# A Delta-rule layer whose TensorE order is written as chains woven with projections

## The chip, the cores and the metric

The kernel runs on one NeuronCore of a Trainium2 chip. The metric is the device time of one execution in microseconds, the median of several runs. All arithmetic is float32; large products are taken as three products of split operands.

## What is computed

A stack of blocks over x of 512 positions x 1024. The third mixer, a gated Delta-rule layer with 8 heads of 128, is the one that matters:

```python
proj = h @ w_in                            # q, k, v, z: 1024 each; beta, a: 8 each
q, k, v = silu(causal_conv(qkv, w_conv))   # 4 taps
q = q * rsqrt(sum(q * q) + EPS) / sqrt(d); k = k * rsqrt(sum(k * k) + EPS)
beta = sigmoid(beta_logit)
g = -exp(a_log) * softplus(a_logit + dt_bias)
# per head and chunk:
decay = where(causal, exp(g_cum_i - g_cum_j), 0)
L = where(strict, (k_beta @ k.T) * decay, 0); T = inverse(eye + L)
u, w = T @ v_beta, T @ (k_beta * exp(g_cum))
# scan over chunks with a state:
v_new = u - w @ state
o = q_dec @ state + qk @ v_new
state = state * exp(g_last) + k_dec.T @ v_new
# behind the scan: o * rsqrt(mean(o * o) + EPS) * w_onorm, times silu(z), then @ w_out
```

The reference's chunks are 64 long; the kernel works on four of 128 to a head.

## The kernel before

`build` runs the layers one after the other; the order of instructions on each engine comes from a scheduler that works with its own estimates, the code setting the data flow. Tiles are 128 partitions x 512.

**Projections.** `fm` (L346) takes one unit of weights: `mm3` (L328 to L330) issues three matmuls `pj` for each of 8 slices of the contraction, 24 to a unit. The three of one slice are called a k-step here. The layer has one unit of 40 columns (the rates beta and a), then for each of heads 0 to 5 the units k, v, q, z, for heads 6 and 7 k, v, q, and the two z units at the end. Each unit's weights are split on the way: ACT writes `whi` (L222), DVE `wlo` (L223). `pj` has three PSUM banks. All else shares four pools: `pa` (two banks), `pb`, `pc` and `po` (one each).

**One head** in `gdn_layer` (L663 on) goes so:
- A broadcast DMA brings the head's gate row `Gb`; POOL forms `dc`, `dT` (L743, L744), ACT exponentiates them (L749, L750) and `Gb` (L751).
- `conv_silu` for k: DVE multiplies the unit's result by the norm (`u`, L717), four taps (L630, L634), ACT takes silu (L719). TensorE turns it (`kt`, L642), ACT squares (L760), DVE sums (`ssk`), POOL takes the root (`rk`, L659), ACT scales (L765); TensorE turns it back (`knt`), ACT copies `knT` (L768), and TensorE forms `kk` (L771).
- `block_inverses` (L856) inverts the diagonal 16 x 16 blocks: ACT copies four pieces `d`, DVE cuts them down (L868, L870), SP writes them to DRAM (`dd`, L872) and reads them back spread out (`lb`, L875), and DVE sweeps 15 steps of four operations on `tmp` (L882) and `X` (L884).
- v: `conv_silu`, `vt`, scaled by ACT. q: `conv_silu`, the sum of squares `ss` in `sumsq_fm`, and `kq`, which DVE multiplies into `dT` (L791).
- `unit_inverse_T` (L887) joins blocks to 32, 64 and 128: `full` on DVE (L902), `Dt`, `z`, `e`, `dz`, `e`, `dz`, `e` on TensorE, with copies `Dm`, `zt` on ACT between them. It was issued behind the last projection by `tc.issue_after(self.last.ins)`.
- The scan, four chunks: `ks` with the state (L810), `r` on DVE (L812), `vn` (L814), its copy on ACT (L816), `ds` (L819), the new state `S` (L822, L824), the outputs `o` (L826, L827). Then `on` on ACT, and, one head later, `ot` and the gate (`finish`).

Behind the last head come the two z units and `out_proj`, whose own weights follow.

Of the kernel before, what the change touches and what calls it, by code (L numbers as in the profile page):

```python
# [18 lines left out]
P = 128  # L19
S = 512  # L20
# [180 lines left out]
class Stream:  # L201
# [32 lines left out]
    def next(self):  # L234
        while self.done < min(self.pos + 1 + self.look, len(self.plan)):
            self.fetch()
        r = self.ready[self.pos]
        self.ready[self.pos] = None
        self.pos += 1
        return r  # L240


class KB:
# [419 lines left out]
    def gdn_layer(self):  # L663
        nc = self.nc
        self.stage = ("pa", 2)
        self.norm_end()
        h, rb, rc = self.h, self.rb, self.rc
        H = 8
        self.stage = ("pa", 2)
        bps = self.small_fm(40, h)  # L670
        rows = self.big("E", shape=[40, S])
        xb = self.big("E")
        nc.vector.tensor_mul(xb[:40], bps[:40], rb[:40])
        nc.gpsimd.memset(rows, 0.0)
        nc.scalar.activation(rows[:8], xb[:8], AF.Tanh, scale=0.5)
        nc.vector.tensor_scalar(rows[:8], rows[:8], 0.5, 0.5, ALU.mult, ALU.add)
        A = slice(32, 40)
        nc.vector.tensor_scalar_add(xb[A], xb[A], self.col("gdt")[A])
        la, lb = self.big("Gb"), xb
        nc.scalar.activation(la[A], xb[A], AF.Abs)  # L680
        nc.scalar.preload_act_table_set("natural_log_exp_and_others")
        nc.scalar.activation(la[A], la[A], AF.Exp, scale=-1.0)
        nc.scalar.activation(la[A], la[A], AF.Ln, bias=1.0)
        ea = self.small([P, 1], "ea")
        nc.scalar.activation(ea[A], self.col("gal")[A], AF.Exp)
        nc.vector.tensor_scalar_max(lb[A], xb[A], 0.0)
        nc.vector.tensor_add(lb[A], lb[A], la[A])
        nc.vector.tensor_scalar(lb[A], lb[A], ea[A], -1.0, ALU.mult, ALU.mult)
        for t in range(NT):
            c = slice(t * P, (t + 1) * P)  # L690
            nc.vector.tensor_tensor_scan(rows[A, c], self.ones[A], lb[A, c], 0.0, ALU.mult, ALU.add)
        Gb = self.bcast_rows(rows[A], H, "Gb")
        gps = self.att("gc")
        for t in range(NT):
            nc.tensor.transpose(gps[:, t * 40:(t + 1) * 40], rows[:, t * P:(t + 1) * P], self.ident[:40, :40])
        gc = self.small([P, NT, 40], "cols", 1)
        nc.vector.tensor_copy(gc, gps[:, :NT * 40].rearrange("p (t c) -> p t c", t=NT))
        ng = self.small([P, NT, H], "ng", 1)
        nc.vector.tensor_scalar_mul(ng, gc[:, :, 32:40], -1.0)
        nb = self.small([P, NT, H], "nb", 1)  # L700
        nc.vector.tensor_scalar_mul(nb, gc[:, :, 0:8], -1.0)
        nbe = self.small([P, NT, H], "nbe", 1)
        nc.scalar.activation(nbe, gc[:, :, 32:40], AF.Exp)
        nc.vector.tensor_mul(nbe, nbe, nb)
        strict = self.con("strict").unsqueeze(1).to_broadcast([P, NT, P])
        causT = self.con("causT").unsqueeze(1).to_broadcast([P, NT, P])
        v4 = lambda a: a.rearrange("p (t d) -> p t d", t=NT)
# [3 lines left out]
        blk = [slice(t * P, (t + 1) * P) for t in range(NT)]  # L711
        os_, g, NZ = [], [], 2

        def conv_silu(i, hd):
            ps = self.fm(h)
            u = us[(3 * hd + i) % 2]
            nc.vector.tensor_mul(u[:, 3:], ps, rb)  # L717
            y = self.conv_taps(u, "gw", i * 8 + hd, 4, f"y{i}", bufs=3)
            nc.scalar.activation(y, y, AF.Silu)  # L719
            return y, u[:, 3:]  # L720

        late = []

        def finish():

            on, z = late.pop()
            old, self.stage = self.stage, ("pc", 1)
            with self.tc.issue_after(self.last.ins):
                ot = self.t4(on, "ot")
            if z is not None:  # L730
                g.append(self.gate(ot, z, self.col("gon")))
            else:
                o = self.big("o", bufs=NZ)
                nc.scalar.activation(o, ot, AF.Copy, scale=self.col("gon"))
                os_.append(o)
            self.stage = old

        for hd in range(H):
            self.stage = ("pa", 2)

            G = Gb(hd, 2)
# [11 lines left out]
            nc.gpsimd.tensor_copy(eg, v4(G)[:, :, P - 1])  # L753

            kT, sq = conv_silu(1, hd)
            if late:
                finish()
            kps = self.t4(kT, "kt")
# [7 lines left out]
            kps = self.t4(kn, "knt")  # L766
            knT = self.big("knT", bufs=3)
            nc.scalar.copy(knT, kps)  # L768
            kk = self.att("kk")
            for t in range(NT):  # L770
                nc.tensor.matmul(kk[:, blk[t]], knT[:, blk[t]], knT[:, blk[t]], start=True, stop=True)  # L771
            for t in range(NT):
                c = blk[t]
                nc.vector.scalar_tensor_tensor(dc[:, c], kk[:, c], nb[:, t, hd:hd + 1], dc[:, c], ALU.mult, ALU.mult)
            X = self.block_inverses(dc)
            nc.gpsimd.tensor_mul(v4(kn)[:, :NT - 1], v4(kn)[:, :NT - 1], kd[:, :NT - 1].unsqueeze(2).to_broadcast([P, NT - 1, P]))

            vT, _ = conv_silu(2, hd)
            vps = self.t4(vT, "vt")
            bv = vT  # L780
            for t in range(NT):
                nc.scalar.activation(bv[:, blk[t]], vps[:, blk[t]], AF.Copy, scale=gc[:, t, hd:hd + 1])

            qT, sq = conv_silu(0, hd)
            e2 = self.small([P, NT], "e2")
            nc.vector.tensor_scalar(e2, self.sumsq_fm(qT, sq), P * EPS, P * EPS * EPS, ALU.mult, ALU.add)
            kq = self.att("kq")
            for t in range(NT):
                nc.tensor.matmul(kq[:, blk[t]], knT[:, blk[t]], qT[:, blk[t]], start=True, stop=True)
            At = dT  # L790
            nc.vector.tensor_mul(At, kq, dT)  # L791
            qd = qT
            nc.gpsimd.tensor_mul(qd, qT, G)
            z = self.silu_z(2) if hd < H - NZ else None
            self.stage = ("pb", 1)
            with self.tc.issue_after(self.last.ins):
                E = self.unit_inverse_T(dc, X)

            self.stage = ("po", 1)
            ops = self.att("o")  # L800
            self.stage = ("pc", 1)
            so = self.small([P, NT], "sso", 2)
            Sx = None
            for t in range(NT):
                c = blk[t]
                if t == 0:
                    rr = bv[:, c]
                else:
                    ks = self.att("ks")
                    nc.tensor.matmul(ks[:, :P], knT[:, c], Sx, start=True, stop=True)  # L810
                    rr = self.small([P, P], "r", 2)
                    nc.vector.scalar_tensor_tensor(rr, ks[:, :P], nbe[:, t, hd:hd + 1], bv[:, c], ALU.mult, ALU.add)  # L812
                vn_ps = self.att("vn")
                nc.tensor.matmul(vn_ps[:, :P], E[:, c], rr, start=True, stop=True)  # L814
                vn = self.small([P, P], "vn", 2)
                nc.scalar.copy(vn, vn_ps[:, :P])  # L816
                if t < NT - 1:
                    ds_ps = self.att("ds")
                    nc.tensor.matmul(ds_ps[:, :P], kn[:, c], vn, start=True, stop=True)  # L819
                    Sn = self.small([P, P], "S", 2)  # L820
                    if t == 0:
                        nc.scalar.copy(Sn, ds_ps[:, :P])  # L822
                    else:
                        nc.vector.scalar_tensor_tensor(Sn, Sx, eg[:, t:t + 1], ds_ps[:, :P], ALU.mult, ALU.add)  # L824
                if t > 0:
                    nc.tensor.matmul(ops[:, c], qd[:, c], Sx, start=True, stop=False)  # L826
# [3 lines left out]
                if t < NT - 1:  # L830
                    Sx = Sn
# [8 lines left out]
            late.append((on, z))  # L840
        finish()
        self.stage = ("pa", 2)
        for o in os_:
            g.append(self.gate(o, self.silu_z(2)))
        self.out_proj(g, "nw3")

    def sumsq_fm(self, src, s):

        nc = self.nc
        nc.scalar.activation(s, src, AF.Square)  # L850
        ps = self.att("ss")
        for t in range(NT):
            nc.tensor.matmul(ps[:, t:t + 1], s[:, t * P:(t + 1) * P], self.ones[:, 0:1], start=True, stop=True)
        return ps[:, :NT]
# [32 lines left out]
    def unit_inverse_T(self, N, X):  # L887
# [3 lines left out]
        nc = self.nc  # L891
        v4 = lambda a: a.rearrange("p (t d) -> p t d", t=NT)
        off = self.small([P, S], "off", 1)
        nc.gpsimd.tensor_mul(v4(off), v4(N), self.con("off16").unsqueeze(1).to_broadcast([P, NT, P]))
        for s in (16, 32, 64):
            X2 = self.big("E", shape=[P, NT, P]) if s == 64 else self.small([P, NT, 2 * s], f"X{2 * s}", 1)
            nc.gpsimd.tensor_scalar_mul(X2[:, :, :s], X, self.con(f"even{s}"))
            if s == 16:
# [4 lines left out]
                                     self.con(f"bd{s}").rearrange("p (b i) -> p b i", i=s).unsqueeze(1).to_broadcast([P, NT, nb, s]))  # L903
                ps = self.t4(full, "Dt")
                Dm = self.small([P, S], "Dm", 1)
                nc.scalar.copy(Dm, ps)
                zp = self.att("z")
# [4 lines left out]
                ep = self.att("e")  # L912
# [3 lines left out]
                nc.vector.scalar_tensor_tensor(X2[:, :, s:], X, self.con(f"odd{s}"), ev, ALU.mult, ALU.add)  # L916
            else:
                nc.scalar.activation(X2[:, :, s:], X, AF.Copy, scale=self.con(f"odd{s}"))
                dz = self.att("dz")
# [10 lines left out]
                ep = self.att("e")  # L930
                for lo, pair in rows:
# [3 lines left out]
                    nc.scalar.copy(X2[lo, :, s:], ep[lo, :w].rearrange("p (t c) -> p t c", t=NT))  # L935
            X = X2
# [597 lines left out]
```

## Time and profile before

| | |
|---|---|
| runs before | 2082.03, 2085.77, 2086.82 us; median 2085.77 |
| profiled execution | 2088.03 us |
| its span | 2086.3 us, mean granted clock 0.989 |
| busy in the span | PE 2026.5, DVE 1213.0, ACT 886.7, POOL 164.3 us |
| the layer on TensorE | 505.7 to 928.0 us, the next layer's norm at its end |

The profile is one execution; the 1.7 us between its time and its span lie around the span. In the trace L12 is line 12 of the kernel; PE is TensorE's matmuls, PEld its weight loads. A view of windows gives the busy time of each engine in a stretch, with the number of instructions, the mean granted clock of TensorE (PEclk, 1.00 is full), and the share of DMA. A releaser behind `<-` is what the waiting instruction waited for last.

The columns of a window are:

```
core 0: us, PE busy (x) PEld busy (x) DVE busy (x) ACT busy (x) POOL busy (x), PEclk, DMA share, GB/s
```

### The profile page before, as it was taken

To read this page: it belongs to the slowest core of one execution; us is meant where nothing else is said; L and a number is where in the kernel's file an instruction comes from. 1 tells how busy PE (TensorE), PEld (TensorE's weight loads), DVE (VectorE), ACT (ScalarE), POOL (GpSimd) and SP (SyncE) were. 2 spreads that over 40 slices of the span, in tenths; PEclk is the share of its full clock that TensorE was granted. 3 is DMA by queue.
4 is the path that set the end of the run, shared out by engine and by line. 5 is a ranking of instruction groups with operands and counts; after the bars stand their busy time and mean duration, and the time that the engine had idled before them with its cause. 6 is when DMAs were issued, how large, how long until landed. Compare 5 with 4: busy or idle time off the path is not lost.

```text
span 2086.3 us, 25930 instructions
## 1 busy us (share of the span) xinstructions
PE 2026.5 (97%) x9810; PEld 1592.0 (76%) x9810; DVE 1213.0 (58%) x2420; ACT 886.7 (43%) x1640; POOL 164.3 (8%) x178
## 2 busy tenths in 40 slices
PE   8999999999899988999999999999999999999999
PEld 6888787777777766778667767776788878888887
DVE  5545445555876765465765546644544467878621
ACT  4222343344776553453565454356622243322211
POOL 0000000000333221100001101000011100000000
PEclk9999999999999997999999999999999999999999
DMA  5233432225322221153114412120232342332331
GB/s 183 92 101 117 137 110 78 85 72 175 87 78 65 65 75 31 52 179 98 50 41 157 123 59 93 61 81 31 71 101 92 99 165 93 99 101 92 111 121 66
DMA packets 64508, 197.69 MB, mean 95 GB/s; under 512 B 8412, under 2 KB 8796, under 8 KB 64384
## 3 DMA queue, kind: packets, MB, share of 16 engines
q1 hardware_dynamic: 63440, 193.57, 28.9%
q0 software_dynamic: 800, 2.25, 0.4%
q8 instruction: 77, 1.26, 0.3%
q14 instruction: 47, 0.39, 0.1%
q10 hardware_dynamic: 144, 0.22, 0.0%
HBM read 183.13 MB, written 12.89 MB: 94 GB/s over the span
## 4 chain that ended last, share of the span: by engine, by line
PE 61%; DVE 5%; ACT 4%; DMA 2%; POOL 2%; issue 1%; POOLq 0%; SPq 0%; ACTq 0%; DVEq 0%
PE pj L330 16%; PE pj L328 16%; PE pj L329 16%; DMA lb<-dd 2%; PE s L1042 1%; PE z L1404 1%; DVE tmp L882 1%; PE o L1095 1%; PE pt L1086 1%; DVE X L884 1%; DVE wlo L223 1%; POOL rk L659 1%; PE dz L926 1%; PE tm L328 0%; PE dz L928 0%
## 5 line engine op out<-in xcount | busy, mean ns | idle before, releaser
L328 PE MATMUL pj<-hh,whi 128*128 128x512 f32 (+2 forms) x1528 | 609.1, 399 | 7.6 <-ACT hh L342 7.6
L329 PE MATMUL pj<-hl,whi 128*128 128x512 f32 (+2 forms) x1528 | 611.2, 400 | 1.2 <-DVE hl L343 1.2
L330 PE MATMUL pj<-hh,wlo 128*128 128x512 f32 (+2 forms) x1528 | 609.3, 399 | 2.0 <-DVE wlo L223 2.0
L222 ACT CAST whi<-raw 128x1024 fp32r<-128x1024 f32 x301 | 313.7, 1043 | 663.9 <-PE pj L329 417.3
L223 DVE TENSOR_TENSOR wlo<-raw,whi 128x1024 fp32r<-128x1024 f32 x301 | 375.5, 1248 | 203.5 <-ACT whi L222 197.2
L328 PEld LDWEIGHTS pj<-hh,whi 128*128 128x128 f32 (+2 forms) x1528 | 288.1, 189 | 68.3 <-ACT hh L342 8.0
L330 PEld LDWEIGHTS pj<-hh,wlo 128*128 128x128 f32 (+2 forms) x1528 | 288.3, 189 | 64.8 <-issue 4.3
L329 PEld LDWEIGHTS pj<-hl,whi 128*128 128x128 f32 (+2 forms) x1528 | 288.4, 189 | 62.7 <-issue 3.6
L328 PE MATMUL pj<-gh,whi 128*128 128x512 f32 x432 | 170.7, 396 | 0.5 <-ACT gh L339 0.3
L329 PE MATMUL pj<-gl,whi 128*128 128x512 f32 x432 | 170.7, 396 | 0.0
L330 PE MATMUL pj<-gh,wlo 128*128 128x512 f32 x432 | 170.6, 396 | 0.0
L634 DVE SCALAR_TENSOR_TENSOR y<-u,cols,y 128x512 f32<-128x512 f32 x160 | 123.0, 769 | 2.4
L328 PEld LDWEIGHTS pj<-gh,whi 128*128 128x128 f32 x432 | 81.0, 188 | 20.4 <-ACT whi L222 1.1
L329 PEld LDWEIGHTS pj<-gl,whi 128*128 128x128 f32 x432 | 81.0, 188 | 18.7 <-DVE gl L340 0.4
L330 PEld LDWEIGHTS pj<-gh,wlo 128*128 128x128 f32 x432 | 81.1, 188 | 18.4 <-DVE wlo L223 0.4
L473 DVE TENSOR_TENSOR x<-pj,x 128x512 f32<-128x512 f32 x48 | 33.1, 691 | 93.9 <-PE pj L330 93.9
L328 PE MATMUL pj<-whi,hh 128*128 128x512 f32 x168 | 66.4, 398 | 0.0
L329 PE MATMUL pj<-wlo,hh 128*128 128x512 f32 x168 | 66.1, 394 | 0.0
L330 PE MATMUL pj<-whi,hl 128*128 128x512 f32 x168 | 65.7, 392 | 0.0
L1435 DVE TENSOR_TENSOR gt<-pj,rb 128x512 f32<-128x512 f32 x24 | 16.5, 690 | 64.1 <-PE pj L330 64.1
L882 DVE TENSOR_TENSOR tmp<-lb,X 128x30 f32<-128x30 f32 (+14 forms) x240 | 43.7, 214 | 11.8 <-DMA lb<-dd 11.8
L1466 DVE TENSOR_TENSOR u<-pj,rb 128x512 f32<-128x512 f32 x44 | 30.5, 693 | 30.5 <-PE pj L330 28.7
(480 smaller groups left out, 2845.1 us busy)
## 6 DMA issues: line engine op xcount, KB each, us to landing
raw<-in_w_dram SPq DMA_DIRECT2D x290, 512.0 KB, 3.5
xd<-x SPq DMA_DIRECT2D x40, 256.0 KB, 2.0
x<-xd SPq DMA_DIRECT2D x40, 256.0 KB, 3.4
x<-in_xT_dram SPq DMA_DIRECT2D x16, 256.0 KB, 3.2
lb<-dd SPq DMA_DIRECT2D x8, 512.0 KB
raw<-in_w4m_dram SPq DMA_DIRECT2D x8, 512.0 KB, 4.0
ncb<-ncb SPq DMA_DIRECT2D x8, 256.0 KB
Gb<-Gb SPq DMA_DIRECT2D x8, 256.0 KB, 3.2
```

The costliest lines, as they stand in the source:

```text
L222: nc.scalar.copy(hi, raw)
L223: nc.vector.tensor_sub(lo, raw, hi.bitcast(F32))
L328: nc.tensor.matmul(out, ah, bh, start=start, stop=False)
L329: nc.tensor.matmul(out, ah, bl, start=False, stop=False)
L330: self.last = nc.tensor.matmul(out, al, bh, start=False, stop=stop)
L473: nc.vector.tensor_add(x, ps, x)
L634: nc.vector.scalar_tensor_tensor(y, u[:, t:t + S], self.col(f"{key}{t}", j), y, ALU.mult, ALU.add)
L659: nc.gpsimd.tensor_tensor(o, m, self.nhalf[:, :n], ALU.pow)
L882: nc.vector.tensor_mul(tmp[:, a, :n], lb[:, j + 1:, a, j].rearrange("p i t -> p t i"), X[:, a, j:j + 1].to_broadcast([P, 2, n]))
L884: nc.vector.tensor_add(X[:, a, j + 1:], X[:, a, j + 1:], tmp[:, a, :n])
L926: nc.tensor.matmul(dz[lo, c], X[pair, t], self.ident[pair, lo], start=True, stop=True)
L1466: nc.vector.tensor_mul(u[:, 2:], ps, self.rb)
```

## The change

The head's work is cut into generators: `norm`, `rates`, `keys` (down to the scan and `ot`), `values`, `queries`, `gates`. Each yields, at the points where it would wait, what its matmuls cost and how long the next ones take to become ready, in us. `Weave` keeps a clock of its own from these numbers: it takes the chain whose time has come first, and else one k-step of the next projection unit at 0.69. When a unit is full its chain begins. `until` asks every 0.7 whether another chain has got so far. All of it stands in `tc.manual_schedule` for PE, so TensorE's order in the layer is the one that the code writes; the other engines' is still the scheduler's.

Beside that: `ot` and the gate follow in the head's own chain (no `late`, no `finish`, no `issue_after`), the two `u` buffers go round by order of use (`turn`), `kq` is written ahead of `ss`, and `ks` is followed at once by `o` of the state. Instructions are the same in number and shape on each engine, but for 41 table loads in the program in place of 45.

```diff
+class Weave:
+    def __init__(self):
+        self.t, self.chains = 0.0, []
+    def begin(self, chain):
+        self.chains.append([self.t, chain])
+        self.step(self.chains[-1])
+    def step(self, c):
+        r = next(c[1], None)
+        if r is None:
+            self.chains.remove(c)
+            return
+        self.t += r[0]
+        c[0] = self.t + r[1]
+    def run(self, filler, cost):
+        more = True
+        while more or self.chains:
+            c = min(self.chains, key=lambda c: c[0], default=None)
+            if c and c[0] <= self.t:
+                self.step(c)
+            elif more:
+                more = next(filler, self) is not self
+                self.t += cost if more else 0.0
+            else:
+                self.t = c[0]
...
+        def until(*keys):
+            while any(k not in done for k in keys):
+                yield 0, 0.7
...
+        def keys(ps, hd):
+            yield from until("rates")
+            gc, ng, nb, nbe = done["rates"]
+            kT, sq = conv_silu(ps, 1, hd)
...
-            kT, sq = conv_silu(1, hd)
-            if late:
-                finish()
-            kps = self.t4(kT, "kt")
+            yield 0, 6.5
+            kps = t4(kT, "pa", 2, "kt")
...
-            kps = self.t4(kn, "knt")
+            yield 0.45, 6.0
+            kps = t4(kn, "pa", 2, "knt")
             knT = self.big("knT", bufs=3)
             nc.scalar.copy(knT, kps)
-            kk = self.att("kk")
+            done["k", hd] = knT, dT, G
+            yield 0.45, 1.5
+            kk = bank("pa", 2, "kk")
...
-            with self.tc.issue_after(self.last.ins):
-                E = self.unit_inverse_T(dc, X)
+            yield 0.9, 21.0
+            E = yield from self.unit_inverse_T(dc, X)
+            yield from until(("v", hd), ("q", hd))
...
+                    nc.tensor.matmul(ops[:, c], qd[:, c], Sx, start=True, stop=False)
+                    yield 0.45, 1.2
...
                 nc.scalar.copy(vn, vn_ps[:, :P])
+                yield 0.22, 1.2
...
                 if t < NT - 1:
-                    Sx = Sn
+                    yield 0.45, 1.2
...
-            late.append((on, z))
-        finish()
+            yield 0.25, 5.0
+            ot = t4(on, "pc", 1, "ot")
...
+        def values(ps, hd):
+            yield from until("rates")
+            gc = done["rates"][0]
+            vT, _ = conv_silu(ps, 2, hd)
+            yield 0, 6.0
+            vps = t4(vT, "pa", 2, "vt")
...
+        def queries(ps, hd):
+            yield from until("rates")
+            qT, sq = conv_silu(ps, 0, hd)
+            nc.scalar.activation(sq, qT, AF.Square)
+            yield 0, 6.5
+            yield from until(("k", hd))
...
+            yield 1.8, 0
...
+        with self.tc.manual_schedule(engines={mybir.EngineType.PE}):
+            weave.begin(norm())
+            weave.run(projections(), 0.69)
...
     def unit_inverse_T(self, N, X):
...
+                self.stage = ("pb", 1)
                 ps = self.t4(full, "Dt")
                 Dm = self.small([P, S], "Dm", 1)
                 nc.scalar.copy(Dm, ps)
+                yield 0.45, 1.2
...
                 nc.scalar.copy(z, zp[:, :NT * s])
+                yield 0.9, 1.0
...
                 nc.vector.scalar_tensor_tensor(X2[:, :, s:], X, self.con(f"odd{s}"), ev, ALU.mult, ALU.add)
+                yield 0.9, 2.0
...
+                yield 1.2, 1.2
...
+                yield 0.7, 2.0
```

The same places in the two orders. First TensorE at head 0 (`y` is a convolution's result, `hh` and `hl` the split input), the program before:

```order
L642 MATMUL kt_4054<-cons_c,y_4048 128x128 x4
...
L642 MATMUL knt_4070<-cons_c,y_4048 128x128 x2
L329 MATMUL pj_4268<-hl_3671,whi_4164 128x512
L642 MATMUL knt_4070<-cons_c,y_4048 128x128 x2
...
L771 MATMUL kk_4077<-knT_4075 128x128 x4
L642 MATMUL vt_4200<-cons_c,y_4194 128x128 x4
```

and the changed program:

```order
L675 MATMUL kt_4143<-cons_c,y_4058 128x128 x4
L675 MATMUL vt_4159<-cons_c,y_4088 128x128 x4
L361 MATMUL pj_4139<-hh_3627,whi_4017 128x512
...
L675 MATMUL knt_4205<-cons_c,y_4058 128x128 x4
L898 MATMUL kq_4212<-y_4126,knT_4210 128x128 x4
L903 MATMUL ss_4218<-cons_c,u_3906 128x1 x4
L816 MATMUL kk_4226<-knT_4210 128x128 x4
```

`vt` moved from behind `kk` to right behind `kt`, and `kq` and `ss` from behind `kk` to ahead of it; `kt` itself has 21 `pj` more ahead of it than before.

Then ACT at head 0, before:

```order
L751 ACTIVATE Gb_3996<-Gb_3996 128x512
L765 ACTIVATE y_4048<-kt_4054,rk_4064 128x128 x4
L719 ACT_TABLE_LOAD
L719 ACTIVATE y_4194<-y_4194 128x512
L768 COPY knT_4075<-knt_4070 128x512
```

and in the changed program (`y_4088` is v's, `z_4189` the gate's, `dc_4338` head 1's):

```order
L795 ACTIVATE Gb_4064<-Gb_4064 128x512
L777 ACT_TABLE_LOAD
L777 ACTIVATE y_4088<-y_4088 128x512
...
L807 ACTIVATE y_4058<-kt_4143,rk_4153 128x128 x4
L793 ACTIVATE dc_4338<-dc_4338,cols_4045 128x128
...
L222 CAST whi_4194<-raw_4192 128x1024
L914 ACT_TABLE_LOAD
L914 ACTIVATE z_4189<-z_4189 128x512
L811 COPY knT_4210<-knt_4205 128x512
```

The silu of v now comes ahead of the key's scaling, and four exponentials of head 1, a split, a load and the gate's silu stand between the scaling and the copy of `knT`.

Last, DVE at the scan of head 4 and the sweep of head 5, before:

```order
L824 SCALAR_TENSOR_TENSOR S_6243<-S_6227,eg_5831,ds_6241 128x128
L630 TENSOR_SCALAR y_6526<-u_3993,cols 128x512
L223 TENSOR_TENSOR wlo_6550<-raw_6547,whi_6549 128x1024
L812 SCALAR_TENSOR_TENSOR r_6251<-ks_6249,nbe_3989,y_6022 128x128
L634 SCALAR_TENSOR_TENSOR y_6526<-u_3993,cols,y_6526 128x512 x3
L834 SCALAR_TENSOR_TENSOR rom_6261<-sso_6205,e_6075 128x4
L882 TENSOR_TENSOR tmp_6385<-lb_6381,X_6383 128x2x15 x2
```

and in the changed program:

```order
L971 TENSOR_TENSOR tmp_6364<-lb_6360,X_6362 128x2x12 x2
L913 TENSOR_TENSOR z_6537<-pj_6470,rb_3959 128x512
L973 TENSOR_TENSOR X_6362<-X_6362,tmp_6364 128x2x12 x2
L853 SCALAR_TENSOR_TENSOR S_6513<-S_6479,eg_5714,ds_6511 128x128
L971 TENSOR_TENSOR tmp_6364<-lb_6360,X_6362 128x2x11 x2
L223 TENSOR_TENSOR wlo_6543<-raw_6540,whi_6542 128x1024
L973 TENSOR_TENSOR X_6362<-X_6362,tmp_6364 128x2x11 x2
L900 TENSOR_TENSOR dT_6144<-kq_6518,dT_6144 128x512
L971 TENSOR_TENSOR tmp_6364<-lb_6360,X_6362 128x2x10 x2
L905 TENSOR_SCALAR e_6529<-ss_6524 128x4
L973 TENSOR_TENSOR X_6362<-X_6362,tmp_6364 128x2x10 x2
L838 SCALAR_TENSOR_TENSOR r_6534<-ks_6532,nbe_4051,y_5824 128x128
```

The whole scan of head 4 stood ahead of head 5's sweep; now its second and third state and what follows stand among the steps of the sweep.

## Rows read from the trace of the kernel before

**Rows 1.** Windows from the layer's start, cut where each `kk` ends; columns as named.
```profile
505.70:543.70 38.00, 33.01 (x147) 24.04 (x146) 27.97 (x45) 23.84 (x39) 12.45 (x15) 0.96 0.33 102
543.70:608.00 64.30, 61.35 (x363) 48.98 (x362) 49.66 (x183) 50.54 (x100) 20.94 (x18) 0.97 0.31 91
608.00:658.10 50.10, 48.43 (x361) 38.40 (x361) 34.84 (x107) 34.55 (x86) 17.09 (x17) 0.97 0.16 49
658.10:696.30 38.20, 34.29 (x177) 27.63 (x177) 29.05 (x100) 26.07 (x61) 10.79 (x10) 0.96 0.29 85
696.30:746.90 50.60, 49.05 (x365) 36.70 (x363) 31.44 (x103) 29.35 (x77) 13.56 (x15) 1.00 0.25 64
746.90:795.10 48.20, 42.51 (x226) 33.65 (x224) 30.75 (x100) 23.25 (x57) 12.15 (x12) 0.81 0.22 61
795.10:834.70 39.60, 33.43 (x170) 26.85 (x170) 24.28 (x91) 14.92 (x41) 6.12 (x5) 0.85 0.16 41
...
sum 422.30, PE 393.65 PEld 305.66 DVE 279.23 ACT 246.93 POOL 104.56; mean PE 43.74 PEld 33.96 DVE 31.03 ACT 27.44 POOL 11.62
```

**Rows 2.** Waits of TensorE in the layer: us in total, times, longest.
```profile
PE knt L642 <- ACT y L765: 6.7, 5, 3.0
...
PE kt L642 <- ACT y L719: 4.2, 1, 4.2
PE vn L814 <- DVE r L812: 4.0, 1, 4.0
...
PE bc L418 <- DVE sq L416: 1.4, 1, 1.4
```

**Rows 3.** Windows around single waits; columns as in rows 1 (PEclk is third from last).
```profile
537.60:541.10 3.50, 2.87 (x9) 2.32 (x10) 3.32 (x5) 3.26 (x7) 1.46 (x3) 0.51 0.03 5
691.70:693.30 1.60, 0.03 (x1) 0.03 (x2) 1.60 (x7) 0.45 (x2) 1.12 (x1) 1.00 0.03 13
693.30:697.00 3.70, 3.70 (x27) 3.28 (x27) 1.92 (x5) 1.81 (x6) 1.54 (x2) 1.00 0.40 142
...
776.60:797.10 20.50, 19.44 (x108) 15.31 (x109) 7.58 (x17) 5.79 (x16) 5.61 (x7) 0.50 0.16 51
```

**Rows 4.** Timeline of TensorE: start, us, engine, line, operation, count.
```profile
514.72 0.39 PE L328 MATMUL pj<-hh,whi 128*128 128x512 f32 x1
514.95 0.39 PE L329 MATMUL pj<-hl,whi 128*128 128x512 f32 x1
...
528.90 0.60 PE L642 MATMUL kt<-cons_c,y 128*128 128x128 f32 x4
```

**Rows 5.** Timeline of ACT at head 0; idle before and its releaser in brackets.
```profile
535.15 0.39 ACT L750 ACTIVATE dT<-dT,ng 128x128 f32<-128x128 f32 x1
535.44 0.61 ACT L751 ACTIVATE Gb<-Gb 128x512 f32<-128x512 f32 x1
537.81 1.14 ACT L765 ACTIVATE y<-kt,rk 128x128 f32<-128x128 f32 x4 [1.75 <-POOL rk L659]
538.97 1.28 ACT L719 ACT_TABLE_LOAD   x1
540.26 0.63 ACT L719 ACTIVATE y<-y 128x512 f32<-128x512 f32 x1
540.80 0.57 ACT L768 COPY knT<-knt 128x512 f32<-128x512 f32 x1
...
541.80 1.03 ACT L222 CAST whi<-raw 128x1024 fp32r<-128x1024 f32 x1
```

**Rows 6.** Timeline of DVE at head 0 (first row) and at head 5.
```profile
527.73 0.69 DVE L717 TENSOR_TENSOR u<-pj,rb 128x512 f32<-128x512 f32 x1
...
759.56 0.32 DVE L882 TENSOR_TENSOR tmp<-lb,X 128x30 f32<-128x30 f32 x2 [3.91 <-DMA lb<-dd]
...
762.08 0.29 DVE L882 TENSOR_TENSOR tmp<-lb,X 128x24 f32<-128x24 f32 x2
...
776.91 0.69 DVE L902 TENSOR_TENSOR full<-X,cons_c 128x512 f32<-128x512 f32 x1
```

## What is predicted

> **What bounds the kernel now.** I read the windows by stretch first, cut at the ends of the `kk` products, then the waits of TensorE, then windows around single stretches for the clock, and last the rows of ACT, DVE and TensorE at two heads.
>
> The layer takes 422.30 us, and TensorE is busy for 393.65 of them, the next engine (DVE) for 279.23 [rows 1]. So TensorE is the bound, by its order: it runs its list one by one, and what it loses is of three kinds.
> - Idle: 422.30 - 393.65 = 28.7 us [rows 1]. The costliest waits are `knt` for the scaled key 6.7, `kt` for silu 4.2, `vn` for `r` 4.0; the norm's broadcast `bc` takes 1.4 [rows 2].
> - Clock: (1 - granted clock) x length over the six of the nine stretches that stand below 1.00 [rows 1] gives 1.5 + 1.9 + 1.5 + 1.5 + 9.2 + 5.9 = 21.6 us (the last two, not shown, stand at 1.00). The clock has two levels there: 0.51 (1.2 GHz) for the 3.5 us around the 3.0 us wait of `knt` at head 0, and 0.50 for 20.5 us behind the 4.2 us wait of `kt`; behind the wait of 1.6 us that ends at 693.3 it stays at 1.00 [rows 2, 3].
> - The rest: small products slower than back to back. A `pj` comes every 514.95 - 514.72 = 0.23 us [rows 4]; the 33 units of 24 alone are 182 us. What small products lose behind each other is in both kernels, as their instructions are the same in number and shape.
>
> So I compare idle plus clock: **50.3 us now**. The change alters the order alone, and can win at most that.
>
> **The change part by part.** No matmul, vector or DMA instruction comes or goes; ACT has four table loads fewer in the whole program (45 to 41), 4 x 1.28 [rows 5] = 5.1 us on an engine busy 246.93 of 422.30 [rows 1]: nothing on the path, except where a silu waits behind a load, and that is counted below. `Weave` fills the gaps of its chains with projection k-steps, so the present waits of `knt`, `ot`, `kt` and `Dt` have work ahead of them, and I take them out. What decides is whether the gaps in the code (6.5 for convolution to `kt`, 21.0 for `kk` to `Dt`, 1.2 in the scan) are as long as the other engines need. TensorE now cannot step aside where one is too short: all projections written behind the waiting matmul wait too, and with them the convolutions, gates and weight splits that they feed. I walked the new order by hand, each instruction starting when its engine was free and its inputs were there, with durations from rows.
>
> 1. *`vt` of head 0.* It stands right behind `kt`, 21 `pj` later than `kt` stood: 528.90 + 21 x 0.23 + 0.60 = 534.3 [rows 4]. Its silu stands on ACT behind the exponentials of the gates: Gb's ends at 536.05, then a load of 1.28 and a silu of 0.63 [rows 5]: 538.0. TensorE waits 3.7. Bounds: 0, and 7.2, since this silu ends 13.2 us after its `u` (527.73 to 540.89) where the code allows 6.0 [rows 5, 6].
> 2. *`kq` and `kk` of head 0.* Behind the key's scaling ACT now has four exponentials (about 0.3 apart, 0.39 each), a split of 1.03, a load of 1.28 and a silu of 0.63 before the copy `knT` of 0.57 [rows 5]: 4.7 us against 0.7 for the four `knt`. Wait 4.0; bounds 0 and 4.7.
> 3. *`Dt` of head 0.* Behind `kk`, 84 `pj` and 16 small products at 0.15 (four `kt` took 0.60 [rows 4]): 84 x 0.23 + 2.4 = 21.7 us. In head 5 the blocks `lb` landed 759.56 - 746.9 = 12.7 us behind `kk`, and `full` was there 777.6 - 746.9 = 30.7 us behind it, the sweep having stood behind other DVE work [rows 1, 6]. Bounds 0 and 30.7 - 21.7 = 9.0; the walk gives 4.0, since less stands on DVE there.
> 4. *`kt` of head 2.* Walk 2.7; bounds 0 and 6.7 (13.2 less the 6.5 planned).
> 5. *Scans of heads 1 and 2.* `ks` 1.5, `vn` 3.1 and 2.3, `e` 2.0: 8.9. Bounds 0 and the present worst, 4.0, for each [rows 2].
> 6. *Heads 4 to 6, alike.* DVE's order puts the state `S` of the scan behind seven rows of the next head's sweep, which begins when `lb` has landed: no earlier than 12.7 + 2.5 us behind `kk` (from 759.56 to 762.08 DVE did so many rows [rows 6]). TensorE reaches `ks` there after 33 `pj` and 24 small products, taken at 0.19, so 7.6 + 4.5 = 12.1 us behind `kk`: wait 3.0. Then `r` behind a `wlo` split 1.0, `kt` behind a table load 1.2, and `e` behind the second `Dm` copy, which stands on ACT behind key scaling that waits for POOL (1.75 at head 0 [rows 5]) 2.0. That is 7.2 a head, 21.6 in all; bounds 0 and 12.
> 7. *Last two heads* 2.0, and 1.9 at the start as now (`bc` 1.4 [rows 2], `gc` 0.5).
>
> Idle then is 3.7 + 4.0 + 4.0 + 2.7 + 8.9 + 21.6 + 2.0 + 1.9 = 48.8 us. Clock: eight stretches like the 3.5 us one, which loses half, 1.7: 13.6. I take the short kind, being the commoner one. Sum 62.4 against 50.3, **+12 us**: the profiled execution of 2088.0 would become 2100. The median shown stands 2.3 us below that execution, so 2098 for the median.
>
> *A rule weighed.* The rows show the silu starting 540.26 - 538.97 = 1.29 us after the load's start [rows 5], so nothing lies between. The Trainium skill, "ScalarE: Activation LUTs", section "What ACT_TABLE_LOAD costs", adds a drain of about 1.38 us to the load's 1.28. With it the five waits above that stand behind a load (`vt`, `kq`, three `kt`) would each be 1.4 longer, and the sum +19; the measured row decides, and I leave it out.
>
> **The rivals.**
> - *The gaps hold* (faster). If DVE gets through the sweep with less in between, `full` comes inside the plan; if TensorE is late at `ks`, `S` is already there. Then items 3, 5 and most of 6 go: idle 3.7 + 4.0 + 2.7 + 5 + 1.9 + 2 = 19, clock 5 x 1.7 = 8.5, together 28 against 50.3: -22.5, 2063. It decides at `ks` of heads 4 to 6: no wait if TensorE comes later than about 15 us behind `kk`. For it: projections are never short until the filler ends. Against: `lb` at 12.7 us and the order on DVE.
> - *No change.* The new waits come at three quarters of my prices, 46.9 x 0.75 + 1.9 = 37, which with the clock's 13.6 is what is lost now: 2086. A form of it, that the change doesn't do what it says, I exclude for TensorE's order: the rows of the new program stand as written, save that the output projections fill in behind the last filler.
> - *The clock stays down* (slower still). About 13 of the new waits are of the size of those that cost clock now. If each costs the present mean (21.6 us over six stretches, 3.6 [rows 1]), clock takes 47, and the sum is 96 against 50.3: +45, 2131. For it: the one wait of 4.2 us was followed by 20.5 us at half clock [rows 2, 3]; against: the wait of 3.0 by 3.5 only. The Trainium skill, "TensorE: Matmul & The Clock Gate", section "HAM oscillation — how this bites in real kernels", tells of a kernel that went back to half clock at every wait between its bursts; the trace agrees for those two waits and not for the one of 1.6.
>
> **How the numbers follow.** The forecast has 0.45: with items 3, 5 and 6 varied by a third (11.5 us) and above the case of no change, 2090 to 2110; the gaps hold 0.28; no change 0.17; the clock 0.10. A measurement of this kernel tells about 0.2% (4.2 us) from no change. Of the case of no change 0.14 falls within that, 0.02 below and 0.01 above: faster 0.28 + 0.02 = 0.30, same 0.14, slower 0.45 + 0.10 + 0.01 = 0.56. The range, 2062 to 2122, leaves out half of the clock rival and the lower half of the first one, 0.05 + 0.14.
>
> **What would show it.** In the new profile TensorE's waits should list `vt` and `kq` in the first 50 us, `ks` behind DVE's `S`, `vn` behind `r`, and `e` behind ACT's `Dm`; `kk` of head 0 should end near 554 instead of 543.7, and the three heads from `kk` 3 to `kk` 6 take about 141 us instead of 137.0 [rows 1]. Half clock should come in short stretches. I am wrong if the layer is under 410 us, if `ks` and `e` don't wait, or if a half-clock stretch of 10 us or more follows most waits.

## The result, and the profile after

The change makes the kernel slower: 2147.47 us (median of 4 runs, 2141.68 to 2151.78) against 2086.3, a ratio of 1.0292 with a 95% interval from 1.026 to 1.0324. The sign was forecast; the size was not: +12 us was said, +61 came, and 2147 lies above the range. The profiled execution took 2141.68 us, its span is 2139.9 against 2086.3, and of the difference of 53.6, 53.3 lies in the layer. These are its windows after the change, cut as in [rows 1] at the end of each `kk`, with two more to the next layer's norm (columns as there):

```profile
505.30:556.90 51.60, 42.67 (x178) 32.50 (x177) 31.17 (x50) 33.61 (x58) 13.58 (x17) 0.85 0.31 100
556.90:625.00 68.10, 56.96 (x339) 46.53 (x339) 48.07 (x178) 33.23 (x79) 18.53 (x18) 0.94 0.24 68
625.00:685.80 60.80, 48.76 (x352) 40.56 (x353) 35.18 (x107) 32.78 (x82) 16.18 (x15) 0.92 0.17 49
685.80:736.20 50.40, 42.49 (x258) 34.63 (x257) 30.86 (x102) 28.09 (x67) 11.87 (x13) 0.90 0.22 59
736.20:789.70 53.50, 44.19 (x264) 36.14 (x263) 29.97 (x101) 27.84 (x65) 11.81 (x12) 0.87 0.20 55
789.70:841.10 51.40, 42.08 (x264) 34.49 (x263) 30.08 (x101) 27.51 (x65) 11.75 (x12) 0.87 0.21 58
841.10:885.80 44.70, 35.59 (x188) 30.52 (x187) 24.79 (x98) 16.11 (x47) 7.44 (x7) 0.81 0.18 48
885.80:942.20 56.40, 52.20 (x370) 40.48 (x369) 23.07 (x95) 21.83 (x64) 7.89 (x8) 0.97 0.13 39
942.20:980.90 38.70, 36.58 (x145) 29.36 (x146) 25.99 (x34) 20.29 (x30) 1.78 (x3) 0.91 0.61 202
sum 475.60, PE 401.51 PEld 325.21 DVE 279.19 ACT 241.28 POOL 100.83; mean PE 44.61 PEld 36.13 DVE 31.02 ACT 26.81 POOL 11.20
```

The layer takes 475.6 us in place of 422.3. Idle time is 475.60 - 401.51 = 74.1 (28.7 before), and (1 - clock) x length over the nine rows is 49.0 (21.6 before). The waits of TensorE in the layer after the change (us in total, times, longest):

```profile
PE ks L836 <- DVE S L853: 16.8, 5, 5.5
PE vt L675 <- ACT y L777: 8.4, 3, 4.8
PE Dt L675 <- DVE full L996: 7.1, 2, 3.9
PE vn L842 <- DVE r L838: 5.0, 2, 2.5
PE e L1033 <- ACT X L1034: 4.5, 8, 1.2
PE dz L1024 <- ACT Dm L1027: 4.2, 7, 1.1
PE e L1033 <- ACT Dm L1027: 4.1, 3, 2.4
PE ks L836 <- DVE gg L487: 3.8, 1, 3.8
PE z L1006 <- ACT Dm L1001: 3.5, 1, 3.5
PE kt L675 <- ACT y L777: 3.1, 3, 1.2
...
PE kq L898 <- ACT knT L811: 2.2, 1, 2.2
PE knt L675 <- ACT y L807: 2.2, 1, 2.2
```

The `knt` of 6.7 is down to 2.2, `kt` from 4.2 to 3.1 [rows 2]. In their place stand the ones that the forecast named, and more of each. The largest stands at head 5's sweep. The timeline of TensorE there, without its projections:

```profile
800.35 1.06 PE L898 MATMUL kq<-y,knT 128*128 128x128 f32 x8
801.24 0.95 PE L903 MATMUL ss<-cons_c,u 128*128 128x1 f32 x8
807.67 0.80 PE L836 MATMUL ks<-S,knT 128*128 128x128 f32 x2 [5.47 <-DVE S L853]
```

And of DVE:

```profile
803.98 0.31 DVE L971 TENSOR_TENSOR tmp<-lb,X 128x30 f32<-128x30 f32 x2 [6.10 <-DMA lb<-dd]
804.22 0.30 DVE L973 TENSOR_TENSOR X<-X,tmp 128x30 f32<-128x30 f32 x2
...
805.57 0.68 DVE L913 TENSOR_TENSOR z<-pj,rb 128x512 f32<-128x512 f32 x1
806.17 1.19 DVE L973 TENSOR_TENSOR X<-X,tmp 128x24 f32<-128x24 f32 x2
807.28 0.33 DVE L853 SCALAR_TENSOR_TENSOR S<-S,eg,ds 128x128 f32<-128x128 f32 x1
```

DVE stands idle for 6.1 us in front of the sweep, whose `lb` comes 14.3 us behind `kk` (789.7), and the state `S`, whose operands were there at 800.3, waits behind the sweep's first rows. TensorE waits for `S`, and everything written behind `ks` waits too. The window 803.8 to 810.5 around it:

```profile
803.80:810.50 6.70, 2.83 (x9) 2.45 (x10) 6.52 (x32) 0.63 (x1) 1.27 (x1) 0.50 0.19 58
```

Half clock for 6.7 us, in more than half of which TensorE was idle anyway.

### The profile page after: what moved, and what is told of

It reads as the page before. It is cut to its first block, busy times and chain, and to the rows that moved or that the text cites. A ratio compares the mean times of both kernels' runs of the same rounds, so it can differ in the third digit from the quotient of the medians.

```text
span 2139.9 us, 25909 instructions
## 1 busy us (share of the span) xinstructions
PE 2035.2 (95%) x9810; PEld 1612.6 (75%) x9810; DVE 1213.6 (57%) x2420; ACT 881.0 (41%) x1636; POOL 160.5 (7%) x178
## 4 chain that ended last, share of the span: by engine, by line
PE 81%; DVE 6%; ACT 5%; DMA 3%; issue 2%; POOL 2%; POOLq 0%; ACTq 0%; DVEq 0%; SPq 0%
PE pj L361 22%; PE pj L362 22%; PE pj L363 22%; DMA lb<-dd 2%; PE s L1142 1%; PE z L1504 1%; PE o L642 1%; DVE wlo L223 1%; PE o L1195 1%; DVE y L667 1%; PE pt L1186 1%; DVE tmp L971 1%; DMA dd<-d 1%; PE tm L361 1%; PE tm L363 1%
## 5 line engine op out<-in xcount | busy, mean ns | idle before, releaser
L361 PE MATMUL pj<-hh,whi 128*128 128x512 f32 (+2 forms) x1528 | 622.2, 408 | 7.1 <-ACT hh L375 7.1
L971 DVE TENSOR_TENSOR tmp<-lb,X 128x30 f32<-128x30 f32 (+14 forms) x240 | 37.4, 190 | 29.1 <-DMA lb<-dd 29.1
L1566 DVE TENSOR_TENSOR u<-pj,rb 128x512 f32<-128x512 f32 x44 | 30.5, 692 | 30.5 <-PE pj L363 28.7
```

The source lines that it names most:

```text
L361: nc.tensor.matmul(out, ah, bh, start=start, stop=False)
L971: nc.vector.tensor_mul(tmp[:, a, :n], lb[:, j + 1:, a, j].rearrange("p i t -> p t i"), X[:, a, j:j + 1].to_broadcast([P, 2, n]))
L1566: nc.vector.tensor_mul(u[:, 2:], ps, self.rb)
```

## The experiments

Theories: (a) the written TensorE order meets operands too early and holds all that is behind; (b) the recast code itself is slower, whoever orders TensorE; (c) the waits are cheap and the clock behind them is what costs. All ratios are to the kernel before, run on the same chip (2085.9 to 2087.9 there); times of runs from different chips are compared by these ratios, and two runs whose intervals overlap are told apart weakly or not at all.

**1. The order back to the scheduler.** Chains and `Weave` stay.

```diff
-        with self.tc.manual_schedule(engines={mybir.EngineType.PE}):
+        if True:
```

> The chains and Weave stay, but TensorE's order in the layer is left to the scheduler again. If the written order is the cause (waits met too early): back near the kernel before, 2076 to 2100. If the recast code itself is (the turns of the pools, the order in which chains hand work to DVE and ACT): it stays at 2135 or more.

Measured 2079.6, ratio 0.9958 [0.9943, 0.9973]. The layer's window:

```profile
504.30:920.70 416.40, 384.76 (x2343) 300.80 (x2342) 278.90 (x864) 245.69 (x560) 100.88 (x105) 0.97 0.27 81
```

The largest of its waits:

```profile
PE vn L842 <- DVE r L838: 4.5, 3, 2.7
PE knt L675 <- ACT y L807: 4.1, 5, 1.2
```

Idle is 31.6. (b) falls: the chains are even 0.4% faster than the kernel before, and the written order costs 68 us. That includes what the scheduler then does with the other engines, whose order it still makes, and which is not the same in the two programs.

**2. The sweep behind the state.** `block_inverses` is cut in two; the sweep is handed over 16 us later on `Weave`'s clock and queued on DVE behind the last `S`.

```diff
-            yield 0.9, 21.0
+            yield 0.9, 16.0
+            if self.lastS is None:
+                X = self.block_sweep(lb, X)
+            else:
+                with self.tc.issue_after(self.lastS.ins):
+                    X = self.block_sweep(lb, X)
+            yield 0, 5.0
...
```

> The DVE sweep is handed over 16 us behind kk and queued behind the scan's last state; the total gap from kk to Dt stays 21. In the trace of the change ks waits 4.6, 5.5 and 5.3 us for a state that stands behind the sweep, each with 6.8 us of half clock about it. If that order on DVE is what these waits come from, they go with half of their clock: 15 + 10 us less, 2120 to 2132. If another wait takes their place (full later, r, Dm): within 5 us of 2147.

Measured 2140.6, 1.0258 [1.0239, 1.0277], nearer to the second case; the interval overlaps that of the change. `ks` waits 0.8 for DVE's `S` in place of 16.8, and this stands at the list's head:

```profile
PE Dt L675 <- DVE full L1008: 28.0, 5, 7.9
PE vt L675 <- ACT y L778: 9.7, 3, 5.2
```

The reading of the 5 us waits was right, and it won little or nothing: `Dt` is late instead, by 28.0 against 7.1.

**3. The wait filled.** Extra products ahead of a state product of heads 3, 4 and 5.

```diff
+                    if t == 2 and hd in (3, 4, 5):
+                        fill = bank("pb", 1, "fill")
+                        for _ in range(30):
+                            nc.tensor.matmul(fill[:, :384], h[0][0][:, :P], h[0][0][:, :384], start=True, stop=True)
                     ks = bank("pc", 1, "ks")
```

> 30 extra products of 384 columns (about 0.16 us each at full clock, 4.9 us) stand ahead of the third ks in heads 3, 4 and 5; their result is not used. If a wait costs only its own length: they lie in the wait, 2145 to 2152. If the clock behind the wait costs as well: the three stretches of 6.8 us go, 10 us less, 2134 to 2140.

Measured 2142.3, 1.0261 [1.0246, 1.0277], between the two. Its first waits:

```profile
PE vn L846 <- DVE r L842: 14.7, 5, 4.4
PE vt L675 <- ACT y L777: 8.5, 3, 4.9
```

Half-clock time in the layer fell from 99.0 to 78.5 us, but `vn` now waited for `r` 14.7 in place of 5.0. It doesn't tell what the clock alone costs.

**4. Head 0's two gaps**, ahead of `vt` and of `kq`.

```diff
-            yield 0, 6.0
+            yield 0, 6.0 if hd else 16.0
...
             yield from until(("k", hd))
+            yield 0, 0.0 if hd else 6.0
```

> Only head 0: vt is allowed 16 us in place of 6, and kq 6 us behind the key. If the written order was too early there, the waits of vt (4.8) and kq (2.2) go, and with them half of two half-clock stretches of 6.8: 10 to 14 us less, 2133 to 2138. If ACT is late anyway and the wait moves to knt, kk or the next head: within 4 us of 2147.

Measured 2136.5, 1.0234 [1.0207, 1.0262]: 11 us less, in the range of the first case, with an interval that touches that of the change. The trace doesn't show that case's mechanism. `vt` and `kq` of head 0 hardly wait any more (4.8 and 2.2 after the change), but its `knt` does:

```profile
PE knt L675 <- ACT y L807: 6.3, 1, 6.3
```

So the wait moved to `knt`, as the second case said, with a half-clock stretch of 6.8 us about it. `kk` of head 0 ends at 552.7 in place of 556.9; the rest of the gain lies behind it, in other heads, and what brought it is not shown.

**5. One number, the gap from `kk` to `Dt`.** First 28, then 35 in place of 21.

```diff
-            yield 0.9, 21.0
+            yield 0.9, 28.0
```

> One number changed in the kernel after: the gap from kk to Dt is 28 us in place of 21 (the trace shows full 24.7 to 32.5 us behind kk). If the order is written against gaps that are too short, the waits of Dt (7.1) go, and the scan comes 7 us later against the next head's sweep, so that the state is there when ks comes (16.8 of waits): with some half clock 15 to 35 us less, 2112 to 2132. If the waits only move to the next place of the chain, as they did from ks to Dt when the sweep was moved: 2138 to 2152.

> Written order, gap from kk to Dt 35 in place of 21 or 28. The trace shows full at most 32.5 us behind kk, so nothing more is won at Dt; if the rest is chain length, heads end later and the filler runs out before the last ones: 2118 to 2135. If 28 was still too short for what follows (r, Dm, the next head's silu): 2095 to 2112.

Measured 2118.0, 1.0154 [1.0135, 1.0173], and 2125.2, 1.0182 [1.0158, 1.0207]. Nearly half of the loss comes back with 7 us of gap, and more gap gives nothing more. The layer's window at 28:

```profile
504.90:955.50 450.60, 389.60 (x2344) 314.02 (x2342) 281.29 (x864) 249.07 (x562) 96.54 (x105) 0.93 0.24 75
```

And its largest waits:

```profile
PE vt L675 <- ACT y L777: 8.6, 4, 5.1
PE vn L842 <- DVE r L838: 8.6, 5, 2.8
PE dz L1024 <- ACT Dm L1027: 6.7, 7, 2.9
PE ks L836 <- DVE S L853: 4.7, 3, 2.2
```

`ks` behind `S` fell from 16.8 to 4.7 and `Dt` is off the list's head, but 61.0 of idle remain, spread over other steps. The layer is 25.0 us shorter than after the change. Idle gives 13.1 of them; half clock fell from 99.0 to 61.4 us in all, of which TensorE was busy for 83.4 and 56.7, and half of that difference is 13.3. By this count waits and clock weigh alike here, and (c), in which the waits are cheap, doesn't hold.

**6. Longer gaps in more places, and both edits together.** With 28: convolution to `kt` and `vt` 9.0 and head 0's gaps (x6); the late sweep (x10); longer gaps between `Dt`, `z`, `e` and `dz` (x14); the filler in single matmuls (x13). Of x14, whose other edits are of the same kind, and x13:

```diff
-                yield 1.2, 1.2
+                yield 1.2, 2.2
...
-            weave.run(projections(), 0.69)
+            weave.run(projections(), 0.23)
```

> Gaps as long as the trace shows them at three places: convolution to kt and vt 9.0, kk to Dt 28, and the two longer gaps of head 0. If short gaps are the whole of it: near or below the kernel before, 2075 to 2105. If a fixed order with fixed gaps can't meet times that vary from head to head (silu came 4.5 to 10.7 us behind its u): 2115 or more.

> Written order, gap from kk to Dt 28, and the sweep behind the scan's state: the two edits that took waits away, together. In the gap-28 run ks still waited 4.7 for the state and vn 8.6 for r. If each wait comes from one gap or one row on DVE: 8 to 15 us below that run's 2118, 2103 to 2110. If the waits only move along the chain as long as the order is fixed: 2113 to 2125.

> Written order, gap 28, and longer gaps inside the joining of blocks (Dt to z 1.8, z to e 1.5, e to dz 2.8, dz to e 2.2). In the gap-28 run dz and e waited about 16.5 us together. If each wait is its own gap's: 2098 to 2110. If waits move on to other places: 2113 to 2125.

> Written order, gap 28, but the filler comes in single matmuls of 0.23 us in place of blocks of three. If the blocks are what makes the written order worse than the scheduler's (a chain's matmul stands up to 0.69 late): 2095 to 2110. If not: within 5 us of the gap-28 run, 2113 to 2123.

Measured 2118.9, 2118.8, 2116.2 and 2127.0 (ratios 1.0155 [1.014, 1.017], 1.0157 [1.0134, 1.018], 1.0142 [1.0125, 1.0159], 1.0197 [1.0178, 1.0217]). None gives more than the one gap of 28; each time the waits stood elsewhere. Single matmuls were worse by 9 us, outside both of their cases. x6 has head 0's gaps as well as the 28, and the 11 us of experiment 4 don't come on top.

**7. A plan that knows DVE's load.** `Weave` keeps one queue of DVE work, and a step comes no earlier than it allows; at least 13 + 10 (x15) or 13 + 15 (x16) from `kk` to `Dt`.

```diff
+        if len(r) > 2:
+            self.dve = max(self.dve, self.t) + r[2]
+            c[0] = max(c[0], self.dve + r[3])
```

> Written order again, but Weave also keeps DVE's time: each convolution, key norm, kk and sweep adds its DVE work (4.2, 1.0, 1.4 and 7.7 us, from the rows) to one queue, and a step's matmuls come no earlier than that queue lets them; kk to Dt 13 + 10 at least, the sweep behind the scan's state. If gaps that are constant, whatever stands on DVE, are what is left of the loss: 2085 to 2105. If not: 2112 to 2130.

> The same with kk to Dt 13 + 15 at least. If the plan with DVE's load is right, 5 us more of slack change little: within 6 us of the run before it. If slack alone is what counts, the one with 28 is better by 8 us or more.

Measured 2129.2, 1.0202 [1.0187, 1.0218], and 2132.2, 1.0213 [1.0193, 1.0233]: worse than the constant 28. The second stayed within 6 us of the first, as the plan had it, but the first lies where the plan was to fail. My reading that the missing load was the rest of the cause isn't borne out by this plan.

**8. The scheduler's order with the same edits.** The late sweep (x7), the gap of 28 (x8), both (x9), and the late sweep in the kernel before, without chains (x12). The first three join the edits of experiments 1, 2 and 5; of x12:

```diff
-            X = self.block_inverses(dc)
+            lb, X = self.block_rows(dc)
...
+            X = self.block_sweep(lb, X)
             self.stage = ("pb", 1)
```

> TensorE's order left to the scheduler, as in the first run (2079.6), and the sweep behind the scan's state. In that run ks waited 3.5 for the state and 3.5 for a gate that stood ahead on DVE. If these are what is left to win: 2070 to 2077. If full becomes late instead, as under the written order: 2080 to 2090.

> TensorE's order left to the scheduler, gap of 28 in Weave. Weave then only sets in which order the code hands work over. If the gaps matter by TensorE's written order alone: within 4 us of 2079.6. If they matter by the order in which DVE and ACT get their work: 5 us or more away from it.

> The scheduler's order with the sweep behind the scan's state (2065.5) and Weave's gap 28 (alone 5 us better than 21 under the scheduler). If the two add up: 2058 to 2063. If the sweep's place already gave what the gap gives: 2063 to 2070.

> The kernel before, with the sweep handed over just ahead of the joining of blocks, behind the head's other DVE work; nothing else. If the gain of the run with the scheduler's order and the late sweep (2065.5) comes from the sweep's place on DVE alone: 2063 to 2073. If it needs the chains as well: 2078 to 2092.

Measured 2065.5 (0.9894 [0.9874, 0.9914]), 2074.7 (0.9946 [0.9928, 0.9964]), 2068.7 (0.9918 [0.9903, 0.9933]) and 2084.1 (0.9994 [0.9985, 1.0003]). x7 beats both kernels, by 22 us and 82 us. x8 lies 4.9 us below x1 and x9 3.2 above x7, both with intervals that overlap, so the longer gap is not shown to matter under the scheduler.

x12 doesn't test the sweep's place. There the scheduler began the sweep 12.7 to 16.8 us behind `kk`, as in the kernel before (12.6 to 17.6), where in x7, which also queues it behind `S`, it begins up to 28.4 behind. Whether a late sweep helps the kernel without chains stays open. x7's layer as one window:

```profile
506.70:907.70 401.00, 380.80 (x2343) 297.18 (x2341) 275.22 (x864) 254.09 (x566) 102.56 (x105) 0.98 0.28 84
```

TensorE of x7 around its first `Dt`:

```profile
581.25 0.39 PE L361 MATMUL pj<-hh,whi 128*128 128x512 f32 x1
582.11 0.66 PE L675 MATMUL Dt<-cons_c,full 128*128 128x128 f32 x4 [0.47 <-DVE full L1008]
582.52 0.48 PE L362 MATMUL pj<-hl,whi 128*128 128x512 f32 x1
```

`full` comes 29.3 us behind head 0's `kk` here and 42.4 behind head 5's, where the written order had 32.2 and 25.6: the chain is not shorter. Yet TensorE loses half a microsecond, because `Dt` stands that close to where `full` comes, with projections up to it. It is so in other heads too: in x7 `Dt` starts within 0.6 us of the end of `full` in seven heads of eight. With the written gap of 28 it starts 5 to 14 us behind it in seven of eight, so that one number is too long there for most heads, while other steps still wait.

## Why the prediction was wrong

- **Right: the mechanism and its places.** Item 1, `vt` of head 0, was put at 3.7 and measured 4.8; item 3, `Dt` of head 0, at 4.0 and 3.2; the table-load waits of `kt` at 1.2 and 1.18 each; `kk` of head 0 ended at 556.9, "near 554" was said. All the waits named as signs came. The three heads from `kk` 3 to `kk` 6 took 155.3 us, and 141 was said. The drain that the Trainium skill, "ScalarE: Activation LUTs", section "What ACT_TABLE_LOAD costs", adds to a load isn't in this trace either: the load began at 537.82, 0.03 behind the end of `Gb`, took 1.28, and the silu began at 539.11.
- **Wrong: the size of idle, 48.8 forecast and 74.1 measured.** The step that failed is the list: waits that are not in it make the excess. They are `vt` and `knt` of head 1 (2.8, 2.2), `ks` for DVE's `gg` (3.8), `z` for `Dm` (3.5), `Dt` of head 6 (3.9), and 15 small waits of `e` and `dz` (4.5 and 4.2) in steps whose gap I took as kept: 24.9 together. The waits in the list came to rather less than their prices. Item 6 came to 19 in place of 21.6: `ks` behind `S` was priced 3.0 a head and took 4.6, 5.5 and 5.3, but `vn` waited for no `r` there, `kt` waited in two heads of the three, and `e` behind `Dm` 1.5 in all in place of 6.0. At `ks` I had TensorE 12.1 us behind `kk`, and it was there 12.5 behind (802.2 against 789.7); but `lb` landed 14.3 behind `kk`, not 12.7 as in the one head that I took it from, and the rows ahead of `S` took 3.3, not 2.5. In the trace of the kernel before, the sweep begins 12.6 to 17.6 us behind `kk` over the eight heads; I had taken nearly the shortest.
- **Wrong: the term for the clock, 13.6 forecast and 49.0 measured.** "Eight stretches like the 3.5 us one" was the step that failed most. There were 18 stretches at half clock in the layer (6 before), 99.0 us long in all: nine of 3.4, seven of 6.8 and two of 10.2. The count was off more than the price: 18 for 8, at a mean of 2.75 us lost for 1.7. The 47 of the rival "the clock stays down" came near, in part by luck: it had 13 waits at 3.6 each. I gave it 0.10, for the one wait that was followed by 3.5 us only; the six stretches of [rows 1], 3.6 a piece, were a little nearer. The section on HAM oscillation that stands beside it ("TensorE: Matmul & The Clock Gate", the Trainium skill) tells of a drop at every wait of its kernel. Here half clock lay at or just behind 13 of the 15 waits of 1.5 us and more; about `vt` of head 1 (2.8) and `vn` of head 2 (2.5) the clock stayed at 1.00.
- **Wrong: that the rest is the same in both kernels.** Idle rose by 45.4 and the term for the clock by 27.4, together 72.8, but the layer by 53.3. One reason is that half-clock time is idle in part (99.0 long, 83.4 busy; 44.4 and 41.4 before), so what it costs beside idle is half of the busy part, and rose by 21.0, from 20.7 to 41.7. The other is that the busy time, less that half, fell from 372.9 to 359.8: 13.1 less, where the prediction had no change. It is 371.5 in x1 and 372.3 in x7, and 361.2 with the gap of 28. Whether small products really cost less in the written order, or waits that lay hidden under the modelled ends of matmuls are open idle now, is not shown.
- **What is shown of the cause.** The written order is the cause (experiment 1); of its 68 us the gap of 21 from `kk` to `Dt` takes 29 (experiment 5), and with it went the waits of `Dt` for `full`, most of those of `ks` for `S`, and over a third of the half-clock time. Waits taken out one by one come back elsewhere on the chain (2, 3, 4, 6).
- **What stays open.** Why a written order with long gaps still lies some 30 us behind the kernel before. Longer gaps, single matmuls and a plan with DVE's load didn't give it back. The number of waits in the waits view points to where it is: 47 after the change, 49 with the gap of 28, 41 to 51 with DVE's load, but 23 before and 25 in x1 and 23 in x7. That the scheduler places each matmul from its own timing of all engines, and is close enough to the chip, fits `Dt` of x7; it was not tried apart. The run that would try it, the scheduler's own TensorE order written down as it is, was not made.

## What to carry to other kernels

An engine that runs in order turns a gap that is estimated too short into a wait of everything behind it, and each wait that is removed uncovers the next. Slack for the worst head at one step (28 or 35 in place of 21) gave back 29 of 68 us here, and no set of constant gaps that was tried gave back more. Before writing an order by hand, hand the same code to the scheduler: here the new code structure was worth 0.4%, 1.1% with one vector stage moved, and the hand-written order lost 2.9%. When waits of some microseconds are forecast, count the small ones too, and price the clock between the shortest stretch and the mean of those that the trace has: here 1.7 and 3.6 us a piece enclosed the 2.75 that came, and the count was further off than either.

## What the runs showed of the hardware

The granted clock fell more often than I expected: with 15 waits of 1.5 us and more there were 18 stretches at half clock (1.2 of 2.4 GHz), of 3.4, 6.8 and 10.2 us. It didn't go wait by wait: two of the 15 had none about them, and some stretches stood at waits of 1.1 to 1.5 us. With the gap of 28 there were 17 such waits and 12 stretches, 61.4 us together; in x7, with 4 such waits, two, 17.1 us together. And more table loads of ACT didn't go with more time: x7, the fastest, has 37 of them in the layer, the change 27 and the kernel before 31. A load cost TensorE time where a silu that it waited for stood right behind it, as in the two `kt` waits of 1.18.
